# A rare loop moved behind the experts, and normed rows with two buffers on ScalarE's queue

## The chip, the core and the metric

The kernel runs on one core of one Trainium2 chip. The metric is the device time of that core in microseconds. The core has a matrix engine (TensorE, PE in the profile), two engines for elementwise work (VectorE, DVE; ScalarE, ACT), GpSimd (POOL) and SyncE (SP), which here only issues DMA transfers. All of them run their own instruction streams and wait for one another by semaphores. PEld is the loading of the stationary operand into TensorE, which runs beside its products.

## The reference

Two transformer blocks run one behind the other on 512 rows of 1024 numbers, in float32. The first has modulated differential attention beside a Fourier mix, and a mixture of experts behind them: each row picks two of 32 experts. The second mixes a stick-breaking attention with a gated delta net, and a last norm follows. The part that matters here is the mixture of experts:

```python
def hier_moe(h, w_rg, b_rg, w_re, b_re, w_gate, w_up, w_down):
    ...
    top_val, top_idx = lax.top_k(e_in, TOP_K)
    gate = p_grp * jax.nn.softmax(top_val, axis=-1)
    expert = grp[:, None] * EXPERTS_PER_GROUP + top_idx
    ...
    def expert_block(args):
        tok, wt, e = args
        xb = h_pad[tok]
        y = (jax.nn.silu(xb @ w_gate[e]) * (xb @ w_up[e])) @ w_down[e]
        return y * wt[:, None]
```

Each expert has three matrices of 1024 x 512 or 512 x 1024, 6 MB together, so all of them make 192 of the some 300 MB that the kernel moves.

## The kernel before

**Stages.** The program is built in this order: the first block's projections, its attention, then a stage that finishes the attention's output and routes the rows (`second`), then the experts (`phase_moe`), then the whole second block, called the tail here, whose first products are `pgm`. In each stage the code doesn't go to the engines directly. A `Recorder` collects the instructions of the stage and `flush()` sends them out in an order that is planned by costs and priorities; it is nearly always the line of this flush, L1098, that the profile names, so groups are told apart by the names of their tiles. `Recorder.before` holds the times at which the plan of one stage leaves the engines, for the plan of the next one; set to two empty tables, it lets the next plan start from nothing.

**Normed rows.** `Norm2.tile` runs for each of four tiles of 128 rows. It sums squares, transposes, forms the router's logits (`pl`, `plt`, `lg`), and lastly writes the row times its norm into `xn`, from where a DMA takes it to the buffer `xnd` in DRAM (L1167 to L1169). `xn` has one buffer, and the store is issued by SyncE. `route` turns the logits into ranks (the place of each row in its expert's list) and gates (`ge`, `ex` and others are its softmax terms).

**Experts.** Each expert has room for 64 rows in a round; two experts make a pair and fill the 128 rows of a tile. For each of the 16 pairs `gather` builds the list of row numbers `idx` and fetches these rows from `xnd` into `xs` by an indirect DMA, which POOL issues. Two pairs are gathered in the stage before, the others in this one. `moe_pair` then transposes the rows (`px`, 8 instructions of TensorE) and scales them into `xT`, multiplies them with gate and up weights (`pgu`, 64 instructions), forms `hs`, transposes that (`ph`, 4) into `hT`, multiplies with the down weights (`py`, 32), splits the result into a high and a low part (`yh`, `yl`), and adds it back to the rows `x` by products with the 0/1 matrix `PT` (`po`, 16, each pair of them added into `x` by VectorE).

**Weights.** `prefetch` loads expert weights into a ring of 18 buffers `we` of 1 MB each; a pair takes 12 of them. A load is issued by SyncE when the products that read the buffer before are done. The first 18 are issued long before the experts begin.

**The loop for further rounds.** If an expert has more than 64 rows, the rows beyond need further rounds. Their count `nrounds` is read into a register on every engine (L1360), and a loop (L1361 to L1371) runs all 16 pairs again for the next 64 rows of each, with weights loaded afresh through one small buffer. With the inputs at hand no expert has so many, and the loop runs zero times; its branches and its barrier, where the engines wait for one another and for the transfers behind them, stay. In the kernel before it stands ahead of the experts' stage. The tail's first instructions are recorded in the same flush as the experts (`last()` in `phase_moe`), so the planner may put them between the last pairs: loads of the first tail weights and of `g_final` (tile `ogT`), the splitting of weights into `w2h` and `w2l`, and the squares `qT` on which the tail's norm and its first products `pgm` rest.

## Time and profile before

| what | value |
|---|---|
| three timed runs | 1382.15, 1383.69 and 1384.94 us, median 1383.69 |
| the profiled execution | 1381.64 us, its span in the trace 1379.8 us |
| TensorE busy | 1274.7 us, 92% |
| VectorE, ScalarE, POOL busy | 811.9 (59%), 483.8 (35%), 121.8 us (9%) |
| moved by DMA | 301.70 MB, 219 GB/s over the span |
| chain that ended last | TensorE 66%, VectorE 5%, all others 1% or less |

The span is what the trace shows from the first to the last instruction; the time of the execution has 1.8 us around it. TensorE's 92% are a mean over stages that differ. The two stages in question are those around the start of the experts, near 350 us, and around their end, near 870 us. Between them DMA runs at the full width of its engines.

### The profile page before, as it was taken

The numbers are of one execution on the slowest core, as the hardware profiler recorded it, in microseconds if no ns is written. First come the engines' busy times: TensorE is split into PE (matmuls) and PEld (weight loads), VectorE is DVE, ScalarE is ACT, GpSimd is POOL, SyncE is SP. The second block draws the span as 40 slices with busy tenths as digits, with TensorE's granted clock in tenths as the row PEclk, the third lists the DMA queues.
The fourth block names the chain that finished last, engine by engine and source line by source line (L and its number), as shares of the span: only waits on it lengthen the run. The fifth ranks groups of instructions, "written<-read, shape, count | busy, mean of one in ns | idle before, by whom it ended". The sixth has DMA issues, their size and how long they took to land.

```text
span 1379.8 us, 18393 instructions
## 1 busy us (share of the span) xinstructions
PE 1274.7 (92%) x7123; PEld 819.6 (59%) x7123; DVE 811.9 (59%) x1610; ACT 483.8 (35%) x994; POOL 121.8 (9%) x122
## 2 busy tenths in 40 slices
PE   5999898985699899999999899799999999999998
PEld 3777676764244444433333333478777777777776
DVE  5788999853134435443433333978544786567774
ACT  4654375313001111111111111357554666246511
POOL 1222310010000000000000000401000100000010
PEclk9999999998799999999999999899999999999999
DMA  9975420069599999999999994321111221221231
GB/s 342 315 270 169 148 58 32 31 253 352 182 407 408 363 407 407 409 409 409 409 408 409 410 408 179 116 95 62 62 63 63 62 62 62 67 86 62 94 135 61
DMA packets 118803, 301.70 MB, mean 219 GB/s; under 512 B 9915, under 2 KB 43812, under 8 KB 102326
## 3 DMA queue, kind: packets, MB, share of 16 engines
q1 hardware_dynamic: 115318, 289.97, 56.0%
q0 software_dynamic: 3392, 10.50, 2.1%
q8 instruction: 57, 0.93, 0.3%
q14 instruction: 36, 0.29, 0.1%
HBM read 294.14 MB, written 6.31 MB: 218 GB/s over the span
## 4 chain that ended last, share of the span: by engine, by line
PE 66%; DVE 5%; issue 1%; ACT 1%; DMA 1%; POOL 0%; POOLq 0%; DVEq 0%; another core or an unknown queue 0%; ACTq 0%
PE pgm L1098 18%; PE pgu L1098 17%; PE py L1098 12%; PE po L1098 4%; PE pbr L1098 3%; PE psv L1098 2%; PE C L1098 2%; PE pso L1098 1%; DVE yt L1098 1%; PE px L1098 1%; PE pZ L1098 1%; PE pY L1098 1%; DMA xs<-xnd,idx 1%; DVE x L1098 1%; PE z L1098 1%
## 5 line engine op out<-in xcount | busy, mean ns | idle before, releaser
L1098 PE MATMUL pgu<-we,xT 128*64 128x512 f32 x1024 | 259.2, 611 | 2.5 <-DVE xT L784 2.3
L1098 PEld LDWEIGHTS pgu<-we,xT 128*64 128x64 f32 x1024 | 86.3, 140 | 138.8 <-issue 130.2
L1098 PE MATMUL py<-we,hT 128*64 128x512 f32 x512 | 136.2, 597 | 4.9 <-ACT hT L1098 3.3
L1098 PE MATMUL pgm<-bl,w2h 128*128 128x512 f32 x352 | 136.0, 406 | 0.0
L1098 PE MATMUL pgm<-bh,w2h 128*128 128x512 f32 x352 | 135.6, 405 | 0.3 <-DVE ogT L1098 0.3
L1098 PE MATMUL pgm<-bh,w2l 128*128 128x512 f32 x352 | 134.5, 404 | 0.4 <-DVE w2l L1098 0.4
L1098 DVE TENSOR_TENSOR x<-x,po 128x512 f32<-128x512 f32 x152 | 96.5, 681 | 60.6 <-PE po L1098 60.4
L1098 ACT ACTIVATE hs<-pgu 128x512 f32<-128x512 f32 x16 | 9.6, 597 | 344.5 <-PE pgu L1098 329.2
L1098 DVE SCALAR_TENSOR_TENSOR yt<-py,gs,gt 128x512 f32<-128x512 f32 x32 | 24.0, 750 | 118.1 <-PE py L1098 110.8
L1098 DVE TENSOR_TENSOR hs<-hs,pgu 128x512 f32<-128x512 f32 x32 | 22.0, 687 | 114.2 <-ACT hs L1098 101.2
L1098 PEld LDWEIGHTS py<-we,hT 128*64 128x64 f32 x512 | 46.3, 136 | 71.0 <-issue 61.8
L1098 PEld LDWEIGHTS pgm<-bl,w2h 128*128 128x128 f32 x352 | 66.2, 189 | 14.6 <-issue 1.4
L1098 PEld LDWEIGHTS pgm<-bh,w2l 128*128 128x128 f32 x352 | 65.9, 188 | 15.1 <-issue 1.2
L1098 PEld LDWEIGHTS pgm<-bh,w2h 128*128 128x128 f32 x352 | 66.0, 189 | 14.2 <-DVE ogT L1098 0.5
L1098 ACT ACTIVATE xT<-px,mod 128x128 f32<-128x128 f32 x67 | 25.2, 456 | 95.4 <-PE px L1098 79.1
L1098 PE MATMUL po<-yh,PT 128*128 128x512 f32 x128 | 44.0, 434 | 14.6 <-DVE yh L1098 14.1
L1098 DVE TENSOR_TENSOR w2l<-w,w2h 128x2048 fp32r<-128x2048 f32 (+1 forms) x26 | 53.0, 2046 | 5.6 <-ACT w2h L1098 5.1
L1098 POOL DMA_INDIRECT xs<-xnd,idx x16 | 16.3, 1021 | 396.4 <-DVE tok L1098 170.4
L1098 PEld LDWEIGHTS po<-yh,PT 128*128 128x128 f32 x128 | 23.2, 194 | 37.7 <-DVE yh L1098 11.8
L1098 PE MATMUL po<-yl,PT 128*128 128x512 f32 x128 | 41.5, 413 | 2.2 <-DVE yl L1098 2.2
L1098 PE MATMUL px<-ident,xs 128*128 128x128 f32 x128 | 20.7, 295 | 24.6 <-issue 21.5
L1098 PEld LDWEIGHTS px<-ident,xs 128*128 128x128 f32 x128 | 14.9, 148 | 37.7 <-issue 31.3
(562 smaller groups left out, 2605.6 us busy)
## 6 DMA issues: line engine op xcount, KB each, us to landing
we<-in_w_gate_dram SPq DMA_DIRECT2D x64, 1024.0 KB
we<-in_w_up_dram SPq DMA_DIRECT2D x64, 1024.0 KB
we<-in_w_down_dram SPq DMA_DIRECT2D x64, 1024.0 KB
ada<-in_w_ada_dram SPq DMA_DIRECT2D x24, 1024.0 KB
w<-in_w_in_dram SPq DMA_DIRECT2D x24, 1024.0 KB
win<-in_w_in_dram SPq DMA_DIRECT2D x8, 1024.0 KB
wout<-in_w_out_dram SPq DMA_DIRECT2D x4, 1024.0 KB
wo<-in_w_out_dram SPq DMA_DIRECT2D x4, 1024.0 KB
```

The costliest lines, as they stand in the source:

```text
L1098: x = op.alts[e][0](*op.args, **op.kw)
```

## The change

Three things change. The tile `xn` gets two buffers in place of one. Its store is issued by ScalarE, on ScalarE's own queue. And the loop for further rounds, with the reset of `Recorder.before` that follows it, is written behind the experts' stage in place of ahead of it. The experts' stage is then planned from the times that the routing stage leaves, and the tail, which before was recorded together with the last pairs from `last()` on, has the loop between its recorded loads and the rest.

```diff
-        xn = rp.tile([128, 8, 128], F32, tag="xn", bufs=1, name="xn")
+        xn = rp.tile([128, 8, 128], F32, tag="xn", bufs=2, name="xn")
         nc.scaled(xn, s.x1[:, t].rearrange("q (p k) -> q k p", k=8), rs[:, t:t + 1])
-        nc.sync.dma_start(s.xnd[128 * t:128 * t + 128], xn.rearrange("q k p -> q (k p)"))
+        nc.scalar.dma_start(s.xnd[128 * t:128 * t + 128], xn.rearrange("q k p -> q (k p)"))
...
-
-    with ExitStack() as st:
-        xp = st.enter_context(tc.tile_pool(name="xg", bufs=1, side=right, reuse_waits="tile"))
-        ps = st.enter_context(tc.tile_pool(name="ps_g", bufs=8, space=PSUM, reuse_waits="tile"))
...
-        n = nc.values_load(s.nrounds[0:1, 0:1], min_val=0, max_val=512)
-        with tc.For_i(0, n, 1):
...
-    Recorder.before = ({}, {})
     with ExitStack() as st:
         s.ringD = st.enter_context(tc.tile_pool(name="ringD", bufs=RING - 17, reuse_waits="tile"))
...
         last()
         s.nc.flush()
         s.nc = nc
+
+    with ExitStack() as st:
+        xp = st.enter_context(tc.tile_pool(name="xg", bufs=1, side=right, reuse_waits="tile"))
+        ps = st.enter_context(tc.tile_pool(name="ps_g", bufs=8, space=PSUM, reuse_waits="tile"))
...
+        n = nc.values_load(s.nrounds[0:1, 0:1], min_val=0, max_val=512)
+        with tc.For_i(0, n, 1):
...
+    Recorder.before = ({}, {})
```

The planner lays out the instructions of the engines anew. Three places matter. The first is ScalarE at the end of the routing stage, the rows of the kernel before with - and those of the changed one with +; `ge` and `ex` are gate terms, and all further rows with + belong to the first expert pair.

```order
 L1098 ACTIVATE ge<-ge 128x16
 L1098 ACTIVATE ex<-ex 128x4
-L1098 ACTIVATE xn<-x_1468,rs 128x1024 x3
-L1360 TENSOR_LOAD nrounds
-L1361 COMPARE_AND_BRANCH
-L1361 UNCONDITIONAL_BRANCH x2
+L1098 ACTIVATE xn<-x_1468,rs 128x1024
+L1098 DMA xnd<-xn 128x1024
+L1098 ACTIVATE xn<-x_1468,rs 128x1024
+L1098 DMA xnd<-xn 128x1024
+L1098 ACTIVATE xT<-px,mod_1480 128x128 x4
+L1098 ACTIVATE hs<-pgu 128x512
```

Three of the four tiles stood behind `ex` on ScalarE; now two do, each with its store right behind it, and the loop is gone from this place.

The second place is TensorE from the second to the third expert pair. In the kernel before, from the second pair's last down products to the third pair's first gate products (`pgt` are products for the gates of a later pair):

```order
L1098 MATMUL py_6351<-we_30_6343,hT 64x512
L1098 MATMUL po<-yl,PT 128x512 x2
L1098 MATMUL po<-yh,PT 128x512
L1098 MATMUL po<-yl,PT 128x512
L1098 MATMUL po<-yh,PT 128x512 x5
L1098 MATMUL po<-yl,PT 128x512 x3
L1098 MATMUL po<-yh,PT 128x512
L1098 MATMUL po<-yl,PT 128x512 x2
L1098 MATMUL po<-yh,PT 128x512
L1098 MATMUL po<-yl,PT 128x512 x2
L1098 MATMUL pgt<-gg,P 128x4 x4
L1098 MATMUL px<-ident,xs 128x128 x8
```

In the changed kernel, from the second pair's last gate and up products to its first down products:

```order
L1098 MATMUL pgu<-we_14_3116,xT 64x512
L1098 MATMUL pgu<-we_14_3117,xT 64x512
L1098 MATMUL po<-yl,PT 128x512
L1098 MATMUL ph<-ident,hs 128x128 x4
L1098 MATMUL px<-ident,xs 128x128 x8
L1098 MATMUL py_3128<-we_20_3118,hT 64x512
```

The third pair's transposes `px` stood behind all down products and all products `po` of the second pair; now they stand ahead of them. At the stage's start, 12 transposes (all of the first pair's and four of the second's) stood ahead of the first `pgu`, and now the first pair's 8 alone do.

The third place is VectorE at the end of the experts. In the kernel before:

```order
L1098 SCALAR_TENSOR_TENSOR yt<-py_6939,gs,gt_1479 128x512
L1098 TENSOR_TENSOR x_1468<-x_1468,po 128x512 x2
L1098 TENSOR_TENSOR yl<-yt,yh 128x512
L1098 TENSOR_TENSOR x_1468<-x_1468,po 128x512 x6
L1098 SCALAR_TENSOR_TENSOR qT_9078,ss_9087<-qT_9078,ogT 128x1024
L1098 TENSOR_SCALAR ss_9086<-ss_9086 128x1
L1098 SCALAR_TENSOR_TENSOR qT_9078,ss_9087<-qT_9078,ogT 128x1024
```

In the changed kernel, behind the last add of expert rows and the (untaken) body of the loop:

```order
L1377 COMPARE_AND_BRANCH
L1377 UNCONDITIONAL_BRANCH
L1098 TENSOR_SCALAR ss_9086<-ss_9086 128x1
L1098 CAST w2h<-w_2560_0_3728 128x512
L1098 TENSOR_SCALAR rr_9089<-ss_9086 128x1
L1098 CAST w2h<-w_2560_4_3729 128x512
L1098 TENSOR_TENSOR w2l<-w_2560_0_3728,w2h 128x512
L1098 TENSOR_SCALAR ss_9086<-ss_9086 128x1
L1098 TENSOR_TENSOR w2l<-w_2560_0_3728,w2h 128x512
L1098 TENSOR_SCALAR rr_9089<-ss_9086 128x1
L1098 TENSOR_TENSOR w2l<-w_2560_4_3729,w2h 128x512
L1098 TENSOR_TENSOR ogT<-ogT 128x1024
```

The sums `qT` followed the last add directly. Now the loop stands between, then the splitting of the first tail weights, and the square of `ogT`, which POOL did before; the loads that these need are issued behind the loop too.

## Rows read from the trace of the kernel before

**Rows 1.** Timeline: start us, length, engine line operation, count, [idle before, releaser]
```profile
326.76 2.28 ACT L1098 ACTIVATE xn<-x,rs 128x1024 f32<-128x1024 f32 x1
...
329.06 0.33 SPq L1098 DMA_DIRECT2D xnd<-xn  x1
...
333.37 2.13 ACT L1098 ACTIVATE xn<-x,rs 128x1024 f32<-128x1024 f32 x1 [4.33 <-DMA xnd<-xn]
...
345.59 1.18 POOL L1098 DMA_INDIRECT xs<-xnd,idx  x1 [26.83 <-SPq L1361]
...
353.11 1.97 PE L1098 MATMUL px<-ident,xs 128*128 128x128 f32 x8 [21.48 <-issue]
...
358.20 1.11 PE L1098 MATMUL px<-ident,xs 128*128 128x128 f32 x4 [3.12 <-DMA xs<-xnd,idx]
...
359.24 3.68 PE L1098 MATMUL pgu<-we,xT 128*64 128x512 f32 x8
...
365.96 0.83 SPq L1098 DMA_DIRECT2D we<-in_w_up_dram  x2
```

**Rows 2.** Stretches: engines' busy us (instructions), then TensorE's clock, DMA share, GB/s
```profile
331.00:353.00 22.00, 0.63 (x6) 0.54 (x5) 1.46 (x6) 4.26 (x2) 1.18 (x1) 0.54 0.67 232
...
359.20:366.00 6.80, 6.80 (x23) 2.35 (x24) 2.76 (x7) 0.00 (x0) 0.00 (x0) 0.67 0.00 0
```

**Rows 3.** The loop's line, 331 to 353: ns min/median/max, first and last start
```profile
L1361 PEldq COMPARE_BRANCH  x1: 6052/6052/6052, 331.8 to 331.8; - x1
...
L1361 DVEq COMPARE_BRANCH  x2: 51/56/61, 332.4 to 333.2; - x2
...
L1361 POOLq EVENT_SEMAPHORE  x2: 17/30/43, 350.9 to 351.0; - x2
...
L1361 SPq COMPARE_BRANCH  x1: 41/41/41, 352.9 to 352.9; - x1
```

**Rows 4.** In the experts: a stretch; waits of 365 to 865: sum, count, longest
```profile
500.00:540.00 40.00, 40.00 (x187) 20.11 (x186) 19.78 (x36) 6.04 (x13) 1.98 (x2) 1.00 1.02 409
...
PE po L1098 <- DVE yh L1098: 14.1, 16, 1.5
...
SPq L1098 <- PE pgu L1098: 109.2, 38, 17.9
```

**Rows 5.** Timeline at the end of the experts and the start of the tail
```profile
814.82 13.80 SPq L1098 DMA_DIRECT2D we<-in_w_down_dram  x4
...
854.73 7.14 PE L1098 MATMUL py<-we,hT 128*64 128x512 f32 x32 [0.78 <-DVE hT L1098]
...
861.89 0.34 SPq L1098 DMA_DIRECT2D ogT<-in_g_final_dram  x1
...
866.02 2.16 POOL L1098 TENSOR_TENSOR ogT<-ogT 128x1024 f32<-128x1024 f32 x1 [134.52 <-DMA sv<-in_w_in_dram]
...
866.34 3.67 DVE L1098 TENSOR_TENSOR x<-x,po 128x512 f32<-128x512 f32 x6
...
866.48 1.20 PE L1098 MATMUL po<-yl,PT 128*128 128x512 f32 x4
...
869.93 1.80 DVE L1098 SCALAR_TENSOR_TENSOR qT<-qT,ogT 128x1024 f32<-128x1024 f32 x1
...
885.51 0.58 PE L1098 MATMUL pgm<-bh,w2h 128*128 128x512 f32 x1
```

**Rows 6.** The gathers, tile `xs`: time from issue to landing
```profile
DMA to landing us min/median/max: 4.5/8.5/8.8
```

**Rows 7.** TensorE's timeline in the experts
```profile
376.38 0.65 PE L1098 MATMUL ph<-ident,hs 128*128 128x128 f32 x4
...
421.34 4.13 PE L1098 MATMUL pgu<-we,xT 128*64 128x512 f32 x18
...
460.03 16.99 PE L1098 MATMUL pgu<-we,xT 128*64 128x512 f32 x64 [2.25 <-DVE xT L784]
...
711.33 3.65 PE L1098 MATMUL pgu<-we,xT 128*64 128x512 f32 x16
```

More of the change, by code (lines that the diff above doesn't have):

```diff
@@ L1354, in phase_moe @@
     with ExitStack() as st:
+        s.ringD = st.enter_context(tc.tile_pool(name="ringD", bufs=RING - 17, reuse_waits="tile"))
+        xp = st.enter_context(tc.tile_pool(name="xm", bufs=2, side=right, reuse_waits="tile"))
+        ps = st.enter_context(tc.tile_pool(name="ps_m", bufs=8, space=PSUM, reuse_waits="tile"))
+        s.nc = Recorder(nc, tc)
+        for x in s.ring:
+            s.nc.tile(x)
+        for e0 in range(0, 32, 2):
+            got = s.got.pop(e0, None)
+            if got is None:
+                got = gather(s, e0, s.rank, s.gx, ps)
+                got += gates(s, e0, got[0], s.gx, ps)
+            moe_pair(s, e0, got, xp, ps, load)
+        last()
+        s.nc.flush()
+        s.nc = nc
+    with ExitStack() as st:
         xp = st.enter_context(tc.tile_pool(name="xg", bufs=1, side=right, reuse_waits="tile"))
@@ L1372, in phase_moe @@
     Recorder.before = ({}, {})
-    with ExitStack() as st:
-        s.ringD = st.enter_context(tc.tile_pool(name="ringD", bufs=RING - 17, reuse_waits="tile"))
-        xp = st.enter_context(tc.tile_pool(name="xm", bufs=2, side=right, reuse_waits="tile"))
-        ps = st.enter_context(tc.tile_pool(name="ps_m", bufs=8, space=PSUM, reuse_waits="tile"))
-        s.nc = Recorder(nc, tc)
-        for x in s.ring:
-            s.nc.tile(x)
-        for e0 in range(0, 32, 2):
-            got = s.got.pop(e0, None)
-            if got is None:
-                got = gather(s, e0, s.rank, s.gx, ps)
-                got += gates(s, e0, got[0], s.gx, ps)
-            moe_pair(s, e0, got, xp, ps, load)
-        last()
-        s.nc.flush()
-        s.nc = nc
 RING = 18
```

## The prediction

> **What bounds the kernel now.** I read the trace in the order of the work around the two places where the loop stands. First the timeline from the router's end to the first expert product [rows 1]. Each of its rows is one instruction or a run of equal ones, with the idle time before it and what ended that. VectorE and ScalarE have the gates early, yet the four normed tiles leave one after the other: `xn` has one buffer, so ScalarE waits 4.33 us at 333.37 for the store of the tile before, and the last tile waits for that one's in turn. The gather of `xs` reads all four and begins only at 345.59. TensorE's first transpose comes at 353.11, the second gather (it stands behind the loop) holds it again until 358.20, and the first expert product starts at 359.24. The table of stretches [rows 2] shows what this costs: in the 22 us from 331 to 353 TensorE is busy for 0.63 us, its granted clock falls to the lower of its two levels (0.54 as a mean; 1.2 GHz against 2.4), and DMA moves 232 GB/s; from 359.2 to 366 DMA moves nothing, because all 18 weight buffers are full and none is free before the first products are done. SyncE issues the next weights at 365.96 [rows 1].
>
> Then the loop itself, which runs zero rounds here [rows 3]. Its branch and semaphores end near 352.9, some 2.0 us after POOL, the last to arrive, saw its gather land (350.9). One row stands out: TensorE's branch over the loop's body took 6.05 us, hidden under the 21 us wait; VectorE's took 0.06 us.
>
> In the experts two things run level [rows 4]. DMA is full (share 1.02, 409 GB/s from 500 to 540), but TensorE waits for weights nowhere: its longest total is 14.1 us for `yh`, while SyncE waited 109.2 us for TensorE's gate and up products to free buffers. The last four weights are issued from 814.82 to 828.6 and, 4 MB at 409 GB/s, need some 10 us more, while the last pair's `py`, which uses them, begins at 854.73 [rows 5]. So TensorE's own path sets the end of this stage, with some 15 us in hand before the stream would. In the same rows tail and experts overlap: SyncE loads `g_final` at 861.89, while expert rows are still to come, POOL squares it at 866.02, VectorE's last add of expert rows ends at 870.01 (866.34 + 3.67), and `qT` has begun at 869.93 without a gap. The first `pgm` follows at 885.51.
>
> **Part 1: normed rows.** Two buffers take ScalarE's wait for the store away, and its queue takes four stores out of SyncE's, where weights stood behind them. But by the order of the built program the last two tiles still stand behind `ex` on ScalarE, which in the trace of before is done when the second `xn` starts at 326.76. So the first of them runs 326.8 to 329.0, the other, at 2.2 us as the rows have it, 329.4 to 331.6, and its store goes out at 331.6. How long a store takes on ScalarE's queue beside a full weight stream, no row shows. Lower end: 4.3 us, from the issue at 329.06 to the waiting `xn` at 333.37. Upper end: 8.5 us, the median landing of the gathers, which move as many bytes, through another queue, mostly under that stream [rows 6]. A gain below 4.3 us is excluded, since half of the old issues landed with DMA at 0.67. I take 6: the weights that SyncE was kept from sending (three of them, 3 MB, at 409 GB/s some 8 us) now run at the same time. The gather then starts at 337.6 rather than 345.59. It landed in 5.3 us (345.59 to 350.9); under load 8.5; I take 7. Transposes begin at about 345. The barrier's 2.0 us no longer lies between, and the second gather follows the first at once, so the first product comes 3.3 us after the first transpose (eight transposes, 1.97 us by the row at 353.11 on the low clock, and some 1.3 for the scaling of the tiles) instead of 6.1. It starts near 348.5: **10.7 us earlier** than 359.24; with both low ends 14, with both high ends 7.
>
> A rule of the Trainium skill speaks against this part: "DMA: Bandwidth & Descriptors", section "Issuing engines are not separate DMA queues", says that transfers of all issuing engines share the same engines, and that a second issuer saves only the time of issuing. By it the upper ends would hold and the lead would be 7. No row read here has a store on ScalarE's queue, so the trace leaves it open.
>
> **Part 2: experts.** The weight stream is freed 6.7 us after the first product (365.96 less 359.24), so it restarts 10.7 us earlier too. TensorE's order changes: before, the second pair's transposes stood ahead of the first pair's products; now the first pair runs alone to its end, and waits more (for `hs`, `hT`, `yh` and `xT`). I add up its row of work; 17.1, 7.1 and 14.6 are read [rows 5, 7], the short waits and groups between are estimates at the rows' pace: 17.1 us from first product to `ph` (376.38), 1.5 to `py`, 7.1 for `py`, 1.3 for `yh`, 3.1 + 0.5 for `po`, 1.1 for `px`, 1.5 for `xT`, 14.6 for the second pair's `pgu` (four times 3.65), 2.2 for its `ph`, 7.1 for `py`: 57, and 3.8 for its rows of `po`, still to do. That is 61 against 62.1 (421.34 less 359.24), so 1 us. The third pair took 38.7 us before (421.34 to 460.03), with every `po` ahead of the next `px` and a pause behind it; the new order gives it the interleaved form of the thirteen pairs that follow, which took 31.4 each ((867.7 less 460.03) / 13, the last `po` ending 1.20 after 866.48). That is 7.3 us. Other pairs keep that form, and I put them at no change. The experts so end 10.7 + 1 + 7.3 = **19 us earlier**, within the 10.7 + 15 that the stream allows. Ends: 7 (high ends of part 1, nothing from the order) and 22.
>
> **Part 3: the loop behind the experts.** Work of the tail that stood beside the last pairs now waits for the barrier: eleven loads, the splitting of the first tail weights, the squares. VectorE has the last add (870.01 on the old clock) and arrives last. Queued behind its wait are the `qT` sums, on which every `pgm` hangs. Release: 2.0 us by the old loop at the low end; if VectorE had to fetch its way over the body as long as TensorE, 6.05 + 2.0 = 8.1. TensorE's own 6.05 us begin some 1.5 us before the last add ends, so it may arrive 4 us behind, less if a free DMA makes it shorter. I take 5, between the two. From the release: 4.1 us for `g_final` to land (861.89 to 866.02, no less in hand now than then, DMA being idle), 1.3 for its square, now on VectorE (an estimate: twice the 0.61 us of a 512 wide add, by 3.67 for six, and a little for its start), and the chain from `qT` to `pgm`. That took 15.6 (869.93 to 885.51) with splits of weights between; a part of these now runs while `g_final` lands, so 14; ends 13 and 15.6. Sum 19.4 behind the release, against 15.5 from the last add before: **5 + 3.9 = 8.9 us lost**; ends 2 + 2.9 = 4.9 and 8.1 + 5.5 = 13.6. Behind the first `pgm` the order of all engines is the old one, so I put the rest at nothing.
>
> Here too a rule of the skill speaks against the change: "Runtime: NRT & Kernel Launch", section "Instruction fetch mechanics", says that a taken branch whose target lies outside the fetched pages waits for a DMA fetch. TensorE's 6.05 us agree, VectorE's 0.06 us do not.
>
> **The sum.** -19 + 8.9 = -10.1. The profiled run took 1381.64 us (span 1379.8 and 1.8 around it), the median of the three others is 1383.69, 2.05 more. So 1371.5 for a run like the profiled one, and **1373.6** beside the median.
>
> **The rivals**, all against the median. (a) *All engines pay for the jump.* The second loop has no 21 us wait to hide a fetch: 13.6 instead of 8.9, -19 + 13.6 = -5.4, 1378.3. For it TensorE's 6.05 us; against it VectorE's 0.06. (b) *The stream sets the experts' end.* If a share of 1.02 means that weights are the limit, the end moves with their restart alone: -10.7 + 8.9 = -1.8, 1381.9. Against it TensorE waits for no weights, and 15 us stand in hand. (c) *The start hardly moves.* The last two tiles stay behind `ex`, stores and gathers take 8.5, the order gains nothing: -7 + 8.9 = +1.9, 1385.6. (d) *Slower: the new order of the experts loses in the middle.* All pairs were laid out anew, and a pair that takes the form of the third one (all `po` first, a pause, then the lower clock) costs 7.3 us. One such pair leaves a gain of 2.8; two decide: -10.1 + 14.6 = +4.5, 1388.2; three give 1395.5. For it: before had one in sixteen without any design against it. Against it: in the new order nearly all pairs show `px` and `po` between `pgu`.
>
> **Chances.** The forecast 55%, with its own range 1366 to 1377.5; (a) 15%, (b) 12%, (c) 8%, (d) 10%. About 0.2%, 2.8 us, is what a measurement of this kernel can tell from none. Faster by more (below 1380.9): the forecast, (a) and a third of (b), 74%; within: most of (b) and half of (c), 13%; slower: the rest, 13%. For 8 in 10 the range runs from the forecast's low end, both low costs (-22 + 4.9 = -17.1, 1366.6), over (a) and (b) to 1384.
>
> **What would show it.** Right: last store on ScalarE's queue issued near 332, first gather near 338, first `pgu` near 348.5, weights again from 355, last add of the experts near 851, first `pgm` some 24 us behind it rather than 15.5. Wrong: a first `pgu` after 353 (part 1), a pair of 38 us beyond the third (part 2), a gap from the last add to `pgm` below 20 or above 29 (part 3), or TensorE waiting for `we`.

## The result and the profile after

The changed kernel takes 1363.08 us (median of four runs, 1362.14 to 1364.65) beside 1382.92 us for the kernel before, a ratio of 0.9864 with a 95% interval of 0.9846 to 0.9881 (the two medians divided give 0.9857, inside it). That is 19.8 us less, about twice the 10.1 us of the forecast, and below the end of the range at 1366. The profiled execution's span fell from 1379.8 to 1361.4 us.

The start of the experts, in the timeline of the changed kernel (columns as in [rows 1]; ACTq is ScalarE's queue of transfers):

```profile
328.88 0.33 ACTq L1098 DMA_DIRECT2D xnd<-xn  x1
...
337.90 1.27 POOL L1098 DMA_INDIRECT xs<-xnd,idx  x1 [21.73 <-DVE PT L1098]
...
344.49 0.16 DVE L1098 CAST idx<-ptk 128x1 int32<-128x1 f32 x1 [4.50 <-DMA xs<-xnd,idx]
...
345.81 1.84 PE L1098 MATMUL ptk<-tokid,P 128*128 128x2 f32 x8 [3.80 <-DVE P L1098]
...
347.51 0.99 PE L1098 MATMUL pgt<-gg,P 128*128 128x4 f32 x4
...
348.37 1.97 PE L1098 MATMUL px<-ident,xs 128*128 128x128 f32 x8
...
350.26 15.05 PE L1098 MATMUL pgu<-we,xT 128*64 128x512 f32 x64
...
355.85 0.80 SPq L1098 DMA_DIRECT2D we<-in_w_up_dram  x2
```

The first expert product starts at 350.26 instead of 359.24 [rows 1]. The gathered rows are there at 344.49, when VectorE's cast of a later list is released by them, yet TensorE transposes them only at 348.37. Between, it makes lists of rows for later pairs (`ptk`, `pgt`).

The experts run from there to VectorE's last add, 837.84 + 3.67 = 841.51; before it was 870.01 [rows 5]. The stage shrank from 510.8 to 491.2 us. Its stretches (columns as in [rows 2]):

```profile
350.30:400.00 49.70, 44.64 (x201) 19.27 (x200) 15.26 (x31) 7.32 (x15) 1.98 (x2) 0.98 0.92 351
400.00:450.00 50.00, 50.00 (x236) 23.87 (x236) 19.49 (x39) 8.82 (x19) 2.98 (x3) 1.00 1.03 408
450.00:797.00 347.00, 331.82 (x1455) 145.68 (x1453) 142.44 (x280) 45.53 (x96) 8.92 (x9) 0.99 1.02 408
```

DMA is full from 400 to 797, with no thinner place in it. In the kernel before, the stretch from 400 to 500 moved 392 GB/s:

```profile
400.00:500.00 100.00, 94.45 (x423) 46.40 (x419) 42.47 (x95) 11.22 (x23) 4.14 (x4) 0.95 0.99 392
```

The end of the experts and the start of the tail, first VectorE and the engines around the loop, and then what the loop's line shows for TensorE's and VectorE's queues:

```profile
837.84 3.67 DVE L1098 TENSOR_TENSOR x<-x,po 128x512 f32<-128x512 f32 x6
...
842.01 0.36 SPq L1098 DMA_DIRECT2D ogT<-in_g_final_dram  x1
...
846.02 0.15 DVE L1098 TENSOR_SCALAR ss<-ss 128x1 f32<-128x1 f32 x1 [4.37 <-DMA sv<-in_w_in_dram]
...
850.66 1.21 DVE L1098 TENSOR_TENSOR ogT<-ogT 128x1024 f32<-128x1024 f32 x1
...
851.93 1.21 DVE L1098 SCALAR_TENSOR_TENSOR qT<-qT,ogT 128x1024 f32<-128x1024 f32 x1
...
866.47 0.63 PE L1098 MATMUL pgm<-bh,w2h 128*128 128x512 f32 x1
```

```profile
L1377 PEldq COMPARE_BRANCH  x1: 3401/3401/3401, 839.4 to 839.4; - x1
...
L1377 DVEq COMPARE_BRANCH  x1: 51/51/51, 841.8 to 841.8; - x1
...
L1377 DVEq EVENT_SEMAPHORE  x12: 49/50/50, 844.6 to 845.7; - x12
```

SyncE and the others go on 0.5 us after the last add. VectorE shows nothing between its branch at 841.8 and its semaphores at 844.6, and its first work comes at 846.02. From the last add to the first `pgm` it is 25.0 us; before it was 15.5 [rows 5]. From there to the end of the span both kernels take the same (494.3 us before, 494.9 after).

### The profile page after: what moved, and what is told of

It is laid out like the page before. It is cut to its first block, busy times and chain, and to the rows that moved or that the text cites. A ratio compares the mean times of both kernels' runs of the same rounds, so it can differ in the third digit from the quotient of the medians.

```text
span 1361.4 us, 18392 instructions
## 1 busy us (share of the span) xinstructions
PE 1268.0 (93%) x7123; PEld 823.2 (60%) x7123; DVE 815.4 (60%) x1611; ACT 481.8 (35%) x994; POOL 119.1 (9%) x121
## 5 line engine op out<-in xcount | busy, mean ns | idle before, releaser
L1098 PE MATMUL pgu<-we,xT 128*64 128x512 f32 x1024 | 255.5, 598 | 0.0
L1098 PEld LDWEIGHTS pgu<-we,xT 128*64 128x64 f32 x1024 | 87.6, 137 | 134.6 <-issue 131.1
L1098 DVE TENSOR_TENSOR x<-x,po 128x512 f32<-128x512 f32 x152 | 96.5, 682 | 86.5 <-PE po L1098 86.4
L1098 PE MATMUL py<-we,hT 128*64 128x512 f32 x512 | 135.8, 597 | 5.4 <-DVE hT L1098 2.8
L1098 PE MATMUL pgm<-bl,w2h 128*128 128x512 f32 x352 | 136.2, 406 | 0.0
L1098 PE MATMUL pgm<-bh,w2h 128*128 128x512 f32 x352 | 135.6, 405 | 0.0
L1098 PE MATMUL pgm<-bh,w2l 128*128 128x512 f32 x352 | 134.7, 405 | 0.4 <-DVE w2l L1098 0.4
L1098 ACT ACTIVATE hs<-pgu 128x512 f32<-128x512 f32 x16 | 9.6, 598 | 338.7 <-PE pgu L1098 338.7
L1098 DVE SCALAR_TENSOR_TENSOR yt<-py,gs,gt 128x512 f32<-128x512 f32 x32 | 24.0, 751 | 119.4 <-PE py L1098 118.8
L1098 PEld LDWEIGHTS py<-we,hT 128*64 128x64 f32 x512 | 45.7, 136 | 69.9 <-issue 61.5
L1098 PEld LDWEIGHTS pgm<-bh,w2l 128*128 128x128 f32 x352 | 66.0, 189 | 15.2 <-issue 1.2
L1098 PEld LDWEIGHTS pgm<-bl,w2h 128*128 128x128 f32 x352 | 66.2, 189 | 14.3 <-issue 1.4
L1098 PEld LDWEIGHTS pgm<-bh,w2h 128*128 128x128 f32 x352 | 66.3, 189 | 13.8 <-issue 0.3
L1098 DVE TENSOR_TENSOR hs<-hs,pgu 128x512 f32<-128x512 f32 x32 | 22.0, 687 | 82.3 <-ACT hs L1098 64.6
L1098 DVE TENSOR_TENSOR w2l<-w,w2h 128x2048 fp32r<-128x2048 f32 (+1 forms) x26 | 54.2, 2085 | 5.6 <-ACT w2h L1098 5.1
L1098 ACT ACTIVATE xT<-px,mod 128x128 f32<-128x128 f32 x74 | 27.8, 458 | 81.5 <-PE px L1098 63.0
L1098 PE MATMUL po<-yh,PT 128*128 128x512 f32 x128 | 44.8, 441 | 11.3 <-DVE yh L1098 10.8
L1098 POOL DMA_INDIRECT xs<-xnd,idx x16 | 16.2, 1014 | 374.4 <-DVE tok L1098 215.8
L1098 PEld LDWEIGHTS po<-yh,PT 128*128 128x128 f32 x128 | 23.9, 200 | 33.6 <-issue 13.4
L1098 PE MATMUL po<-yl,PT 128*128 128x512 f32 x128 | 42.7, 415 | 1.2 <-DVE yl L1098 1.2
L1098 ACT ACTIVATE ada<-ada,sc 128x256 f32<-128x256 f32 x69 | 29.8, 501 | 16.8 <-DMA ada<-in_w_ada_dram 16.8
L1098 ACT ACTIVATE p<-sp,mx 128x768 f32<-128x768 f32 x32 | 28.8, 904 | 13.4 <-PE pt L1098 7.1
```

Of the source, the lines that this page charges most:

```text
L1098: x = op.alts[e][0](*op.args, **op.kw)
```

## The experiments

Two theories stood against each other. Theory O: the stage got shorter because TensorE's instructions stand in another order, and they do so because the plan now starts from the times that the routing stage leaves, where before it started from nothing. Theory P: the stage got shorter because its start was earlier and undisturbed. The first four kernels separate the place of the loop, the edit of the normed rows, and the times that the plan starts from. (Where an edit adds lines ahead of the flush, the flush is at L1099 or L1101 in place of L1098.)

**e1: the loop back in front.** Against the changed kernel:

```diff
+    (the loop, L1354 to L1371 of the kernel before)
+    Recorder.before = ({}, {})
     with ExitStack() as st:
         s.ringD = ...
...
-    (the loop, and the reset behind it)
```

> The changed kernel with its loop back ahead of the experts, so that of the change only the two buffers of xn and ScalarE's queue are left; the plan of the experts starts from nothing again. Theory O (most of the 19.6 us by which the experts' stage got shorter comes from the new order of instructions, and that from a plan that starts at the times the routing stage leaves): the order is the old one, first expert product near 352 instead of 359.2, the experts' stage about 505 to 511 us long, last add near 860, no loss behind it; about 7 us faster than the kernel before, 1376. Theory P (the stage got shorter because its start was earlier and undisturbed, whatever the order): the stage shrinks to about 495, and the time is 1363 to 1366.

Measured: 1371.40 us, ratio 0.9932 (0.9910 to 0.9954).

**e2: the loop moved, nothing else.** The kernel before with the loop and its reset behind the experts; `xn` with one buffer, stores by SyncE.

> The kernel before with its loop moved behind the experts and nothing else; xn keeps one buffer and SyncE's queue. Theory O: gather at 345.6 as before, first expert product near 355 (4 us earlier, the barrier and the second gather no longer between), experts' stage near 492 us, 9.5 us lost at the loop behind it: about 14 us faster than before, 1369. Theory P: a late start keeps the stage at about 508, and 9.5 are lost behind it: 1385 to 1387.

Measured: 1366.87 us, ratio 0.9899 (0.9879 to 0.9918).

**e3: the plan from nothing.** Against the changed kernel:

```diff
+    Recorder.before = ({}, {})
     with ExitStack() as st:
         s.ringD = ...
```

> The changed kernel, but the plan of the experts starts from nothing, as it did before: one line that sets the carried times to empty tables ahead of the experts. No instruction is added or taken away. Theory O: the old order comes back (12 transposes ahead of the first gate product), the first product comes near 352, the stage is about 508 us long, and the loop behind it costs 9.5: no gain, 1381 to 1386. Theory P: as the changed kernel, 1363 to 1366.

Measured: 1377.92 us, ratio 0.9972 (0.9958 to 0.9985).

**e4: loop in front, plan from the routing stage's times.** As e1, without the line `Recorder.before = ({}, {})`.

> The changed kernel with its loop ahead of the experts, but without the line behind the loop that sets the carried times to empty tables, so that the experts are planned from the times of the routing stage. Theory O: new order, first product near 352, experts' stage near 492 us, and no loop behind it: last add near 844, first pgm 15.5 us behind it; 1355 to 1358, faster than both kernels. Theory P: as e1 with what the place of the loop gives, no faster than the changed kernel: 1363 to 1376.

Measured: 1366.70 us, ratio 0.9884 (0.9859 to 0.9909).

The marks read from the timelines of all runs, in us (first `pgu`; first `ph`; end of the last add; stage, from first `pgu` to last add; from the last add to the first `pgm`), with the median time:

| run | pgu | ph | last add | stage | to pgm | time |
|---|---|---|---|---|---|---|
| before | 359.24 | 376.38 | 870.01 | 510.8 | 15.5 | 1382.92 |
| changed | 350.26 | 366.26 | 841.51 | 491.2 | 25.0 | 1363.08 |
| changed, again (e15) | 349.12 | 364.62 | 839.07 | 489.9 | 25.0 | 1364.12 |
| e1 loop in front | 350.89 | 366.76 | 859.12 | 508.2 | 15.5 | 1371.40 |
| e2 loop alone | 354.40 | 370.89 | 844.07 | 489.7 | 24.9 | 1366.87 |
| e3 plan from nothing | 348.02 | 364.16 | 856.87 | 508.9 | 25.0 | 1377.92 |
| e4 front, new plan | 358.07 | 373.89 | 855.27 | 497.2 | 15.5 | 1366.70 |
| e5 as e4, lists held | 351.30 | 368.35 | 849.49 | 498.2 | 15.5 | 1358.84 |
| e6 changed, lists held | 345.43 | 361.33 | 843.38 | 497.9 | 25.0 | 1365.31 |
| e7 no loop | 352.88 | 369.69 | 845.10 | 492.2 | 20.3 | 1362.34 |
| e8 short body | 349.30 | 366.39 | 846.10 | 496.8 | 22.4 | 1361.63 |
| e9 changed, heavy stream | 350.57 | 366.57 | 860.27 | 509.7 | 24.9 | 1382.35 |
| e10 before, heavy stream | 357.52 | 373.50 | 869.04 | 511.5 | 15.5 | 1384.21 |
| e11 tail from experts' times | 352.31 | 369.18 | 844.32 | 492.0 | 23.0 | 1362.87 |
| e12 stores by SyncE | 348.71 | 364.34 | 844.35 | 495.6 | 24.9 | 1366.84 |
| e13 transposes first | 355.04 | 372.77 | 849.70 | 494.7 | 24.9 | 1371.19 |
| e14 as e4, transposes first | 359.17 | 376.72 | 852.73 | 493.6 | 15.5 | 1365.32 |
| e16 first products first | 346.08 | 371.72 | 849.92 | 503.8 | 25.0 | 1375.45 |
| e17 as e4, products first | 350.14 | 376.21 | 853.37 | 503.2 | 15.5 | 1365.22 |

Theory O holds. One line without any instruction of its own (e3) makes the stage 508.9 us long, at an earlier start than that of the changed kernel; without that line and with a late start (e2) it is 489.7. Where the loop stands does not matter for the length: e1 and e3 are alike, and so are e2 and the changed kernel. Theory P falls. The times of e1, e2 and e3 came 2 to 5 us below what theory O had (1376, 1369, 1381 to 1386); it is the lengths of the stage that tell the theories apart. The old order is told by the 12 transposes ahead of the first product, which the kernel before, e1, e3 and e10 have and the others don't. The ends of the stage in the timelines, first of e3 and then of e2 (VectorE's last adds come last):

```profile
348.02 12.55 PE L1098 MATMUL pgu<-we,xT 128*64 128x512 f32 x51
...
853.20 3.67 DVE L1098 TENSOR_TENSOR x<-x,po 128x512 f32<-128x512 f32 x6
```

```profile
354.40 6.05 PE L1098 MATMUL pgu<-we,xT 128*64 128x512 f32 x20
...
840.40 3.67 DVE L1098 TENSOR_TENSOR x<-x,po 128x512 f32<-128x512 f32 x6
```

e3 starts 6.4 us ahead of e2 and ends 12.8 us behind it.

The four runs also price the loop's move by itself. From e1 to e3 the experts keep the old order, and the loop goes behind them, with the tail planned from nothing as in the changed kernel: the first product comes 2.9 us earlier, the way to `pgm` gets 9.5 longer, and the time rises by 6.5 us. The move that the change is named after is a loss; what it carries along, a plan that begins elsewhere, is the larger gain. From the kernel before over e1 and e3 to the changed kernel the three parts can be priced one after the other, by the medians: the normed rows 11.0 us faster (1371.40 beside 1382.43 for the kernel before, run along with e1), the loop's move 6.5 slower, the plan that starts from the routing stage's times 14.8 faster.

e4 missed its 1355 to 1358 by 8.7 us, in two places. Its first product came at 358.07, since the lists stood ahead of the transposes, and with the loop in front of both they can't begin before it ends:

```profile
348.01 1.01 PE L1098 MATMUL ptk<-tokid,P 128*128 128x2 f32 x4 [18.69 <-issue]
...
356.17 1.97 PE L1098 MATMUL px<-ident,xs 128*128 128x128 f32 x8
```

And one pair, from its `ph` to the next pair's, took 37.5 us where the changed kernel took 32.6, with the same instructions of TensorE in the same order, in a stretch where the granted clock fell to 0.76 as a mean (the third value from the end is the clock, ahead of DMA's share and rate):

```profile
620.00:640.00 20.00, 20.00 (x70) 7.43 (x70) 5.57 (x12) 0.00 (x0) 0.99 (x1) 0.76 1.02 403
```

**e5 and e6: lists held.** While the lists of the third to sixteenth pair are recorded, they are made to depend on the first pair's scaled rows:

```diff
+                s.nc.hold = (s.xT0,)
                 got = gather(s, e0, s.rank, s.gx, ps)
                 got += gates(s, e0, got[0], s.gx, ps)
+                s.nc.hold = ()
```

> As e4 (loop ahead of the experts, experts planned from the routing stage's times), and the lists of rows of the third to sixteenth pair are held back until the first pair's rows are scaled, so that they no longer stand ahead of the first transposes on TensorE. In e4 the first transpose could have begun at 348.1 (it did in e1) and began at 356.2. If that order alone cost the start: first transpose near 348.2, first expert product near 350.3, stage 491 to 497 us, first pgm 15.5 us behind the last add, 1352 to 1359. Rival (the lists are needed that early, later gathers come late for their pairs): the stage grows by as much as the start gains, 1364 to 1368.

> The changed kernel with the same hold on the lists of the third to sixteenth pair, loop behind the experts. The first gather's rows were there at 344.5, the first transpose began at 348.4. If the lists ahead of it cost that: first transpose near 344.6, first product near 346.6, stage 491 to 495, 25.0 from the last add to pgm, 1359 to 1363. Rival (lists needed early): 1363 to 1367.

Measured: e5 1358.84 us, ratio 0.9834 (0.9817 to 0.9850), the lowest median of all, though its interval still touches that of the changed kernel; e6 1365.31 us, ratio 0.9887 (0.9871 to 0.9904). The first products came within 1.2 us of where they were expected, at 351.30 and 345.43. But the plan laid out the later pairs anew, too, and the stage took 498 us in both. e6 shows it without the loop's place in between: started 4.8 us earlier than the changed kernel, it ended its experts 1.9 us later. It is not that later gathers came late, as the rival has it: in neither trace does TensorE's `px` wait for a gather behind the first pair. From the second pair on e5 and e6 have the same order on TensorE, so they price the loop's move once more: e6 is slower by 6.5 us between the medians, and its first `pgm` comes 3.3 us later.

**e7 and e8: what the loop costs behind the experts.** e7 leaves the loop out; e8 has `range(0, 2, 2)` in its body in place of `range(0, 32, 2)`.

> The changed kernel with the loop left out altogether (further rounds are left out; no expert needs one here); all else in its order. It measures what the loop costs behind the experts. If the barrier keeps the tail's loads, sums and weight splits from standing beside the last pair: the 25.0 us from the last add to the first pgm go back to 15.5 to 17, 1353 to 1355. If only the release of VectorE, 4.3 us, is its price: 1359.

> The changed kernel with only the first pair in the loop's body (further rounds of the other 15 pairs are left out; none is needed here), so that the jump over the body is some 15 times shorter. If the 2.75 us in which VectorE shows nothing behind its branch at 841.8, and TensorE's branch of 3.40 us, are the price of jumping over a long body: both fall below 1 us, first pgm 22 to 23 us behind the last add, 1360 to 1361. If they belong to the barrier whatever the body: 25.0 us and 1363.

Measured: e7 1362.34 us, ratio 0.9855 (0.9836 to 0.9873); e8 1361.63 us, ratio 0.9846 (0.9823 to 0.9870). By the times alone neither is told from the changed kernel; the traces tell more. In e7 the way from the last add to `pgm` is 20.3 us, not 15.5 to 17 but near what the second expectation comes to (25.0 less 4.3); its time is above 1359 since its first `ph` came 3.4 us later than that of the changed kernel. Of the 9.5 us lost, 4.7 go with the loop, and 4.8 stay. In e8 it is 22.4, and the loop's line shows why:

```profile
L1377 PEldq COMPARE_BRANCH  x3: 101/187/310, 843.3 to 846.5; - x3
...
L1377 DVEq COMPARE_BRANCH  x2: 41/46/51, 846.4 to 847.8; - x2
...
L1377 DVEq EVENT_SEMAPHORE  x12: 49/50/50, 846.6 to 847.7; - x12
```

With a body some 16 times shorter TensorE's longest branch took 0.31 us instead of 3.40, and VectorE's semaphores follow its branch by 0.2 us instead of 2.8. So a jump over a long body costs VectorE some 2.6 us, and the time stands not in the branch's row but in the gap behind it. Both agree with what the Trainium skill says in "Runtime: NRT & Kernel Launch", section "Instruction fetch mechanics", that a taken branch out of the fetched pages waits for a fetch. No row shows the fetch itself.

**e9 and e10: a heavier stream.** What limits the experts in either order? Both kernels got more weight traffic, with TensorE's order as it was:

```diff
             for op, e in order:
                 x = op.alts[e][0](*op.args, **op.kw)
+                if (a load of the gate weights in the experts' stage):
+                    op.fn((next of four small tiles), op.args[1][:, 0:1, 0:256])
```

> The changed kernel with a heavier weight stream: behind each of 57 gate loads SyncE issues one more load of 128 KB of weights into a small tile that nothing reads, 7.5 MB in all, 18 us at 409 GB/s; TensorE's order is the same. In the changed kernel the last weights are issued at about 812 and their products begin at 826, so with some 10 us for the landing only some 4 us stand in hand. If the stream sets the end of the experts by now: the stage gets 14 to 18 us longer, 1377 to 1382. If TensorE's own row of work sets it and the order alone shortened the stage: 4 us or less, 1363 to 1367.

> The kernel before with the same heavier stream, 18 us more of DMA. If TensorE's row of work set the end of the experts there, with some 15 us in hand before the stream: 0 to 6 us longer, 1382 to 1388. If the stream set the end already then: 14 to 18 us longer, 1396 to 1400.

Measured: e9 1382.35 us, ratio 1.0005 (0.9995 to 1.0014) to the kernel before, so 19.3 us above the changed kernel; e10 1384.21 us, ratio 1.0022 (1.0009 to 1.0035). The same 18 us of DMA cost the new order 18.5 us of stage and the old order 0.7. So the old order had about as much in hand before the weight stream as was added, and the new order next to nothing. The stretches between full start and end, first of e9 and then of e10:

```profile
400.00:820.00 420.00, 397.81 (x1723) 174.18 (x1722) 162.57 (x318) 54.49 (x116) 11.87 (x12) 0.98 1.03 406
```

```profile
410.00:836.00 426.00, 401.51 (x1753) 176.96 (x1753) 172.41 (x350) 52.81 (x110) 13.13 (x13) 0.98 1.03 406
```

DMA is full in both, and busy shares are alike, so these rows could not have told the two apart. The waits do tell which of the two comes first. What TensorE's loads (PEld) waited for expert weights from 350 to 870, sum, count and longest, is in e9

```profile
PEld pgu L1099 <- DMA we<-in_w_gate_dram: 9.2, 7, 3.5
PEld py L1099 <- DMA we<-in_w_down_dram: 3.4, 7, 1.2
PEld pgu L1099 <- DMA we<-in_w_up_dram: 1.8, 2, 1.4
```

and in the changed kernel no more than

```profile
PEld pgu L1098 <- DMA we<-in_w_gate_dram: 0.2, 1, 0.2
```

Up to the ninth pair e9 keeps the changed kernel's pace to 0.1 us a pair; from there on its pairs are up to 4.2 us longer. So in the changed kernel TensorE's own row still sets the end of the experts, and the weight stream stands right behind it; in e9 the stream sets it.

**e11: the tail planned from the experts' end.** The changed kernel without the reset behind the loop.

> The changed kernel without the line behind the loop that sets the carried times to empty tables, so that the tail is planned from the times at which the experts end; its order is then the old one, with the qT sums first. Of the 9.5 us lost from the last add to the first pgm, the run without a loop (e7) left 4.8, and its tail had the order planned from nothing. If that order is the cause of these 4.8: first pgm 20 to 21.5 us behind the last add instead of 25.0, 1358 to 1360. If the barrier and the late loads decide, whatever the order: 24 to 25 us, 1362 to 1364.

Measured: 1362.87 us, ratio 0.9861 (0.9840 to 0.9883). The way to `pgm` is 23.0 us, between the two expectations. So the tail's order is worth some 2 us of the 9.5 with the loop there, and the times do not tell e11 from the changed kernel.

**e12: SyncE's queue again.** The changed kernel with `nc.sync.dma_start` for the stores and two buffers.

> The changed kernel with the stores of xn on SyncE's queue again, two buffers, loop behind the experts: it measures ScalarE's queue. In the changed kernel the last store took 9.0 us from its issue on ScalarE's queue (328.9) to the gather (337.9), where a store on SyncE's took 4.3 before. If the queue is what makes it long: the gather starts up to 4 us earlier, unless the store stands behind weights on SyncE. If stores share the transfer engines with the weights whatever the queue: a store takes 8 to 9 us here too, and standing behind weights the last one goes out 0 to 8 us later; gather at 338 to 345, time 1362 to 1370.

Measured: 1366.84 us, ratio 0.9896 (0.9875 to 0.9917). The gather began at 334.90, 3.0 us earlier than in the changed kernel. The gather's place alone says little: with instructions that are the same up to there, the gather of the changed kernel, of e15, of e7 and of e8 stands at 337.90, 336.29, 340.03 and 336.30. But these shift with the issue of the last store; from that issue to the gather it is 8.6 to 10.5 us in all fifteen traces with stores on ScalarE's queue, and here 6.3:

```profile
328.65 0.32 SPq L1098 DMA_DIRECT2D xnd<-xn  x1
...
334.90 1.18 POOL L1098 DMA_INDIRECT xs<-xnd,idx  x1 [20.30 <-DVE idx L1098]
```

DMA was full in both (405 GB/s in the 8 us behind the issue here, 424 in the changed kernel), and the gather's last wait here was for its list, so the store itself took no longer than that. The first of the two expectations holds: beside a full stream ScalarE's queue costs the gather 2.3 us or more, as far as the one trace with SyncE's queue tells. The later pairs were laid out differently once more (stage 495.6), and that is why the time is longer all the same.

**e13 to e17: start and order apart.** e13 and e14 move only the first pair's transposes and their scaling ahead of the lists (in the changed kernel and in e4); e16 and e17 move its 64 gate and up products as well. All other instructions keep their order. e15 is the changed kernel once more. In the line below `first` is set on the instructions that are to move:

```diff
         total, order, end, (free, dma) = plan
+        order.sort(key=lambda x: not x[0].first)
```

> The changed kernel with one thing moved: the first pair's 8 transposes and their scaling stand ahead of the lists of later pairs on TensorE and VectorE; every other instruction keeps its place. Run e6 also let the first product come 4.8 us earlier, with the lists planned anew, and the experts ended 1.9 us later. If the layout of the later pairs took that gain away, and the stream (restarted as much earlier) sets the end otherwise: first transpose near 344.7, first product near 346.7, last add 3 to 4 us earlier than 841.5, 1359 to 1360. If an earlier start is worth nothing because the experts' end hangs on something later: last add near 841.5 again, 1362 to 1364.

> As e4 (loop ahead of the experts, experts planned from the routing stage's times) with the same one thing moved; no other instruction changes its place. If the lists ahead of the transposes cost e4 its start, and the end follows the restart of the stream by 484 to 492 us as in e2, e4, e5 and the changed kernel: first transpose near 348.2, first product near 350.2, stream again near 356, last add 840 to 848, first pgm 15.5 us behind, 1352 to 1360. If e4 was slow for another reason (its two slow pairs in the middle): 1362 to 1366.

> The changed kernel once more, on the same chip as e13 and e14, for a direct comparison: 1362 to 1365, last add 484 to 486 us behind the restart of the stream.

> The changed kernel with the first pair's transposes and its 64 gate and up products ahead of the lists of later pairs; all other instructions keep their order. In e13 the lists came to stand between the transposes and the products, and the first product was later, not earlier; here they stand behind the products, where they take TensorE some 7 us ahead of the first ph. If the end of the experts hangs on the restart of the stream (last add 484 to 488 us behind it, as in the changed kernel, e2, e7, e11 and e13): first product near 346.5, stream again near 352, last add near 838, 1358 to 1361. If TensorE's row counts too: the 7 us of lists show in the end, 1364 to 1367.

> As e4 (loop ahead of the experts, experts planned from the routing stage's times) with the same order of the first pair. If the end hangs on the restart of the stream: first transpose near 348, first product near 350.3, stream again near 356, last add 840 to 844, first pgm 15.5 us behind it, 1351 to 1356, the fastest of all. If TensorE's row counts too: 1357 to 1362.

Measured: e13 1371.19 us (ratio 0.9920, 0.9903 to 0.9937), e14 1365.32 (0.9881, 0.9861 to 0.9901), e15 1364.12 (0.9873, 0.9857 to 0.9890), e16 1375.45 (0.9955, 0.9940 to 0.9970), e17 1365.22 (0.9901, 0.9865 to 0.9937). None was clearly faster than the kernel that it starts from, and e13, e16 and e17 lie above both of their expectations. In e13 and e14 the lists came to stand between the transposes and the products, which I had not looked at. In e16 the first product came at 346.08 and the stream was on at 351.57, 4.3 us ahead of the changed kernel, and yet the experts ended 8.4 us later. The lists stood ahead of the first `ph`, which came 5.5 us later than in the changed kernel, behind a wait for `hs`. TensorE's granted clock was at its lower level there, and the down products took 9.69 us instead of 7.14:

```profile
371.72 1.09 PE L1101 MATMUL ph<-ident,hs 128*128 128x128 f32 x4 [3.79 <-DVE hs L1101]
373.59 9.69 PE L1101 MATMUL py<-we,hT 128*64 128x512 f32 x32 [0.78 <-DVE hT L1101]
```

```profile
366.00:376.00 10.00, 5.43 (x20) 3.65 (x21) 3.06 (x7) 0.00 (x0) 0.00 (x0) 0.50 1.01 398
```

So the second pair's `ph` comes at 407.00 where the changed kernel has it at 398.55, first e16 and then the changed kernel:

```profile
407.00 0.66 PE L1101 MATMUL ph<-ident,hs 128*128 128x128 f32 x4 [0.52 <-DVE hs L1101]
```

```profile
398.55 0.66 PE L1098 MATMUL ph<-ident,hs 128*128 128x128 f32 x4 [0.52 <-DVE hs L1098]
```

These 8.45 us are the whole of the 8.4 at the end. The stream lost bytes as well, since the first pair gave back its buffers late:

```profile
346.00:400.00 54.00, 45.41 (x198) 22.29 (x199) 18.55 (x46) 4.87 (x11) 1.98 (x2) 0.85 0.72 268
```

The changed kernel's row for the same length of time has 354 GB/s:

```profile
350.30:404.00 53.70, 48.64 (x221) 20.90 (x222) 16.30 (x34) 8.83 (x19) 2.98 (x3) 0.98 0.93 354
```

86 GB/s less over 54 us is 4.6 MB, at 409 GB/s 11 us of stream. But TensorE's loads waited for expert weights no more in e16 than in the changed kernel, 0.2 us, so this loss does not show in the time.

So neither the restart of the stream nor its lost bytes set the end in these runs, but the time at which TensorE comes to the second `ph`. From there on ten kernels have the same instructions of TensorE in the same order (changed, e4, e7, e8, e11, e13 to e17). In seven of them it is 442.7 to 443.1 us from the second `ph` to the last add. The other three differ by the clock: 441.7 in e15, 446.0 in e8 and 449.1 in e4, with a granted clock from 570 to 670 of 0.98, 0.93 and 0.90 as a mean, beside 0.97 in the changed kernel. With the old order (before, e1, e3) it is 466.3 to 467.5.

## Why the prediction was right and wrong

The direction was right, and the mechanism of parts 1 and 3. The step that failed is in part 2: "Other pairs keep that form, and I put them at no change". The new order of the experts was put at 8.3 us (1 + 7.3) and brought 19.5; those other pairs alone brought 10.5, and e2 and e3 show that the new order hangs on the times which the plan starts from.

- **Part 1**, 10.7 us earlier forecast, 9.0 measured. The last store left at 328.88, 2.7 us before the 331.6 I had worked out, since the gates were ready sooner. It took 9.0 us to the gather, where I took 6 and had 8.5 as the upper end; here the rule of the Trainium skill that I had set against the change ("DMA: Bandwidth & Descriptors", "Issuing engines are not separate DMA queues") fits the row, and by e12 the choice of the queue is 2.3 us or more of these 9.0. The gather landed in 6.6 (7 taken), and the first product came 1.9 us behind the first transpose (3.3 taken). What I did not see are the lists ahead of the first transposes: 3.9 us. That 9.0 came so near to 10.7 is partly luck, since what came earlier than worked out made up for most of what came later.
- **Part 2**, 19 us earlier forecast, 28.5 measured. Of this 9.0 is the start. The first pairs gave more than I thought: up to the fourth `ph` 26.7 us were gained (451.32 beside 478.02), 16.6 of them after the first `ph`, where I had 8.3. From there to the seventh 8.5 were given back (543.93 beside 562.09). That is no wait for weights: the intervals hold lists and transposes of later pairs (the longest 26 list products and 16 transposes), and TensorE waits in them for 0.7 us in all. The seventh to the fifteenth took 252.0 us instead of 262.5 and brought 10.5: these are the pairs that I had put at no change. I had read 31.4 us a pair as the pair's own pace. It is none: a pair whose waits are covered takes 26 to 27 us in both traces, and 12 loads of 1 MB take 30.8 at 409 GB/s. 31.4 is a mean of intervals with only their own pair's work in them and intervals with lists, waits for `yh` and `hs`, or a fallen clock. Two pairs of the changed kernel, by TensorE's transposes, one covered (26.8 us) and one not (32.7 us):

```profile
420.81 1.09 PE L1098 MATMUL px<-ident,xs 128*128 128x128 f32 x8
...
447.62 1.09 PE L1098 MATMUL px<-ident,xs 128*128 128x128 f32 x8
...
640.73 0.66 PE L1098 MATMUL ph<-ident,hs 128*128 128x128 f32 x4 [0.78 <-DVE hs L1098]
...
673.39 0.66 PE L1098 MATMUL ph<-ident,hs 128*128 128x128 f32 x4
```

- **The bound.** I had worked out that TensorE's own row was behind the stream by some 15 us; e10 agrees (18 us of load added, 0.7 us of stage). From it I took 25.7 us as what the stream allows, and that was wrong: the experts ended 28.5 us earlier. The stream itself came on faster. It restarted 10.1 us earlier, but the issue of the last weights ended 14.0 us earlier (814.6 beside 828.6), and from 400 to 500 it moved 407 GB/s instead of 392. By the same reckoning as before, 10 us for the landing, the changed kernel's last `py` at 826.02 has 1.4 us left of the 15:

```profile
797.85 16.71 SPq L1098 DMA_DIRECT2D we<-in_w_down_dram  x4
...
826.02 7.14 PE L1098 MATMUL py<-we,hT 128*64 128x512 f32 x32 [0.78 <-DVE hT L1098]
```

A range that began at the bound of 25.7 and the low cost of part 3, at 1362.9, would have held the result, but by luck: part 2 brought 2.8 us more than that bound, and part 3 lost 4.6 more than its low end.
- **Part 3**, 8.9 us lost forecast, 9.5 measured. Release of VectorE 4.3 to 4.5 us (5 taken, for the reason given: its jump), from there to `pgm` some 20.5 (19.4 taken). Some splits that I had put behind the barrier ran ahead of it, but those that remained stood ahead of the square, and e7 and e11 show that the order of the tail, now planned from nothing, has a share that I had not seen as a term of its own. "Behind the first `pgm` nothing" was right to 0.6 us.
- **Rivals.** (a), that the jump costs, is true in kind: 2.6 us at VectorE (e8). That VectorE's branch row shows 0.06 us was no argument against it, since the cost stands behind the row. (b) did not come: TensorE waited for weights for 0.2 us. But it was near, since the new order left the stream next to nothing in hand (e9). (c) did not come. (d), pairs of the third pair's form, came in no pair of the changed kernel (longest 34.7 us).

What I called the change, the place of the loop, costs 6.5 us (e1 to e3). The normed rows pay for that, and what makes up the larger part of the gain, 14.8 us (e3 to the changed kernel), is a line that I mentioned and did not price: the reset of the carried times no longer stands between the routing stage and the experts' plan. Why a plan that starts from those times fits better was not tried apart; the runs show only that it does.

## What to carry to other kernels

Where a planner lays out the work, ask of a moved block first what the plan starts from on either side of it, and price the new order as a term of its own; its bound is what the next resource allows, here the DMA stream, and that can get faster with the order too. Where two resources run level, busy shares and rates don't tell them apart; the waits tell which one comes first, and a known load added to the other tells how much that one has in hand. A rare loop costs its barrier wherever it stands, so put it where the engines wait anyway; ahead of the experts it cost 2.9 us (e1, e3), and behind them 9.5.

## What the runs showed of the hardware that I had not expected

A jump over a long loop body cost TensorE 6.05 us ahead of the experts, with DMA at a share of 0.67 as the mean from 331 to 353 [rows 2, 3], 3.40 us behind them, where DMA was all but idle (0.02 from 838 to 843), and 0.31 over a short body; VectorE's cost, 2.8 us, is no row of the profile but a gap behind the branch. A store of 512 KB beside a full weight stream took 8.6 to 10.5 us from its issue on ScalarE's queue to the gather that waited for it, in fifteen kernels, and 6.3 on SyncE's queue, where the next weights were issued behind it (e12). In the kernel before, with DMA less full, it was 4.3 and 4.4 on SyncE's queue for the second and the last store (a share of 0.88 and 0.79 meanwhile). Why the queue makes this difference was not tried.
